# Roots on GpSimd, freely ranked modulations, and a context output that leads the second block

## The chip, the cores and the metric

The kernel runs on one core of one Trainium2 chip. The metric is the device time of one execution in microseconds (us), taken as the median of several runs; lower is better. A core has five instruction streams that run at the same time and meet through semaphores: PE (TensorE, matmuls; its weight loads are shown apart as PEld), DVE (VectorE), ACT (ScalarE), POOL (GpSimd) and SP (SyncE, which here issues the DMAs).

## The reference

All arrays are 32-bit floats; there are 256 tokens of width 1024. The program is two blocks of two layers each, one after the other, cut here to what matters:

```
def first_block(x, mem, ...):                  # DEPTH = 2
    for l in range(2):
        h = rms_norm(x, norm_mix_g[l])         # y * rsqrt(mean(y*y) + 1e-6) * g
        z = h @ w_in[l]                        # three branches: recurrent, mLSTM, memory attention
        ... convolutions, scans, attention ...
        x = x + merged @ w_out[l]
        h2 = rms_norm(x, norm_ffn_g[l])
        x = x + (swiglu(h2, ffn_w1, ffn_w3, ffn_w2) if l == 0 else moe_swiglu(h2, ...))   # 8 experts, 2 per token
    return rms_norm(x, final_norm_g)

def second_block(x, c, ctx, c_ctx, ...):       # DEPTH = 2
    for l in range(2):
        mod_x = split(silu(c) @ ada_w[l] + ada_b[l], 6)       # shift, scale, gate, twice
        mod_c = split(silu(c_ctx) @ ada_w[l] + ada_b[l], 6)
        h_x = rmsnorm(x, g) * (1 + mod_x[1]) + mod_x[0]; h_c likewise from ctx
        o_x, o_c = mixer_ab(h_x, h_c, ...) if l == 0 else mixer_c(h_x, h_c, ...)
        x = x + mod_x[2] * o_x; ... swiglu ...; ctx likewise, for l == 0
    return rmsnorm(x, final_g)
```

In mixer_ab four heads are differential attention (an rms norm over each head's output) and four are neighbourhood attention with a bias table; `o_c = [a_c, b_c] @ w_out_ab` is the context's output, from context tokens alone.

## The kernel before

**Tiling.** Activations lie transposed, features on the 128 partitions, in eight tiles of 256 tokens. Every weight comes from HBM as a block of 1 MB (`load`, L136, issued on SP) into a `raw` buffer; `split` (L144) makes two parts of half a block each, `hi` by a cast on ACT (L149) and `lo = raw - hi` on DVE (L150), and a product is three matmuls (hi by hi, hi by lo, lo by hi; L171 and L175, L190 to L192 where two halves go side by side). There are three `raw` buffers for the whole kernel (`rawps0`) and two more while the experts run (`rawp1`, through `more_raw`), with `self.rawps` the list that `load` goes round.

**Order.** The body is traced in program order, and a scheduler puts each engine's instructions in their final order when the kernel is built: it follows a timeline of its own, and gives an engine that is free the ready instruction of highest rank, where rank is the place in program order. `high_priority(offset=n)` moves the rank of what it encloses forward by n instructions. `issue_after(i)` queues what it encloses, on i's engine, behind i. What is traced inside an `If` stays inside, and what is traced outside can't be mixed into it.

**Roots.** `rsqrt` (L213) computes 1/sqrt(v) for columns of at most [128, 4]: an integer operation for a first guess (L218) and seven more steps on DVE, each waiting for the one before. `spread` (L229) lays a column of 128 values along the free axis of all partitions: a diagonal matrix on DVE (L235), multiplied by ones on PE (L236), one diagonal for each of two groups of 128 tokens. `rms` (L255) and `norm` (L261) use both for every norm; `ctx_tile`, `diff`, `enter` and `leave` use `rsqrt` too.

**Modulations.** `ada_layer` (L1134) makes silu(c) and silu(c_ctx), and `ada(n)` (L1149) takes n of 48 chunks of `ada_w`, transposed: a 512 KB load into one of two `adaw` buffers on SP, and one DVE instruction of 1024 columns for each of c and c_ctx (L1163). The first layer's chunks are traced along the first block's mixers and its feed-forward, the second layer's along the second block's first feed-forward. They stand inside `issue_after(self.last_lo.ins)`, that is, behind the DVE half of the last split traced before them.

**Experts.** `moe` (L1057) runs the eight experts for up to 128 tokens each. Behind them every engine reads the largest count of tokens (L1118) and branches (L1119): if it is over 128, a second body of up to eight more experts follows. With the given inputs it is not, and the body is skipped.

**The second block's first mixer.** `mixer_ab` (L1599) loads the first three quarters of `w_out_ab` (`raw`, FILL = 3), then calls `enter` (L1188), which squares x on ACT (L1197), sums on PE (L1201, 32 small matmuls), takes a root and a spread, and makes the norm `h1`. Three units of the context's output (`ctx_out`, 48 matmuls each, from `o_ctx`, ready since the experts' time) follow, then the heads, woven so that one head's dense products fill the waits of another. `rope` (L1230) ends in one POOL multiply (L1238); `na_bias` (L1441) loads a bias by DMA and, on POOL, multiplies it by 8 (L1455) and adds a mask (L1456).

## Time and profile before

| what | us |
|---|---|
| median of 3 runs (3191.67 to 3192.84) | 3192.14 |
| the profiled execution, its own time | 3190.43 |
| its span, first to last instruction | 3188.6 |
| PE busy in the span | 3094.2 |
| DVE, ACT, POOL busy | 2480.8, 1852.6, 70.1 |
| HBM read | 700.38 MB |

The profile is one execution. A line of the timeline gives the start from the span's beginning, the duration (of several instructions together where xN stands at the end), the engine, the line of the kernel, the operation, out<-in with the program's names, and in brackets the idle time of the engine ahead of it and what ended that. A q behind an engine's name is its instruction queue. The last instruction of the span ends 1.8 us short of the execution's own time.

### The profile page before, as it was taken

To read this page: it belongs to the slowest core of one execution; us is meant where nothing else is said; L and a number is where in the kernel's file an instruction comes from. 1 tells how busy PE (TensorE), PEld (TensorE's weight loads), DVE (VectorE), ACT (ScalarE), POOL (GpSimd) and SP (SyncE) were. 2 spreads that over 40 slices of the span, in tenths; PEclk is the share of its full clock that TensorE was granted. 3 is DMA by queue.
4 is the path that set the end of the run, shared out by engine and by line. 5 is a ranking of instruction groups with operands and counts; after the bars stand their busy time and mean duration, and the time that the engine had idled before them with its cause. 6 is when DMAs were issued, how large, how long until landed. Compare 5 with 4: busy or idle time off the path is not lost. (4 is left out here: it accounts for less than half of the span.)

```text
span 3188.6 us, 53070 instructions
## 1 busy us (share of the span) xinstructions
PE 3094.2 (97%) x21140; PEld 2838.1 (89%) x21140; DVE 2480.8 (78%) x3619; ACT 1852.6 (58%) x2612; POOL 70.1 (2%) x102
## 2 busy tenths in 40 slices
PE   8999999999899999999999999999998999989999
PEld 8899999999899898888888888887988999987999
DVE  7668866678778669999999999997876876676555
ACT  5446644444458457887778878776654222256444
POOL 0000000000000000000000000000320000010000
PEclk9999999999999999999999999999998999999999
DMA  7354656555445559999999999997643444430353
GB/s 273 130 175 159 217 179 219 210 193 213 165 160 180 187 188 345 351 344 348 349 347 335 356 344 341 349 346 241 189 115 128 172 165 166 161 127 31 133 185 119
DMA packets 130873, 712.30 MB, mean 223 GB/s; under 512 B 23352, under 2 KB 35000, under 8 KB 53816
## 3 DMA queue, kind: packets, MB, share of 16 engines
q1 hardware_dynamic: 122552, 701.48, 61.0%
q0 software_dynamic: 8064, 7.34, 1.4%
q8 instruction: 167, 2.74, 0.3%
q14 instruction: 90, 0.74, 0.1%
HBM read 700.38 MB, written 1.05 MB: 220 GB/s over the span
## 5 line engine op out<-in xcount | busy, mean ns | idle before, releaser
L149 ACT CAST hi<-raw 128x1024 fp32r<-128x1024 f32 x1192 | 1233.5, 1051 | 829.7 <-PE ps_a L171 356.6
L150 DVE TENSOR_TENSOR lo<-raw,hi 128x1024 fp32r<-128x1024 f32 x1192 | 1426.5, 1221 | 352.2 <-ACT hi L149 340.0
L171 PE MATMUL ps_a<-hh,hi 128*128 128x256 f32 x2128 | 525.0, 283 | 0.2 <-DVE ks L1261 0.2
L171 PE MATMUL ps_a<-hl,hi 128*128 128x256 f32 x2128 | 524.4, 283 | 0.1
L171 PEld LDWEIGHTS ps_a<-hh,hi 128*128 128x128 f32 x2128 | 401.2, 189 | 4.1 <-issue 2.4
L171 PEld LDWEIGHTS ps_a<-hl,hi 128*128 128x128 f32 x2128 | 401.0, 188 | 3.9 <-issue 3.5
L974 PE MATMUL ps_a<-hi,xsh 128*128 128x512 f32 x896 | 355.0, 396 | 0.0
L975 PE MATMUL ps_a<-hi,xsl 128*128 128x512 f32 x896 | 353.9, 395 | 0.0
L976 PE MATMUL ps_a<-lo,xsh 128*128 128x512 f32 x896 | 351.7, 397 | 0.0
L175 PE MATMUL ps_a<-hh,lo 128*128 128x256 f32 x2128 | 299.3, 282 | 0.0
L175 PEld LDWEIGHTS ps_a<-hh,lo 128*128 128x128 f32 x2128 | 273.8, 188 | 0.5 <-issue 0.4
L825 PE MATMUL ps_b<-gh,lo 128*128 128x256 f32 x752 | 212.3, 283 | 0.0
L824 PE MATMUL ps_b<-gl,hi 128*128 128x256 f32 x752 | 212.1, 283 | 0.0
L823 PE MATMUL ps_b<-gh,hi 128*128 128x256 f32 x752 | 210.5, 283 | 0.0
L975 PEld LDWEIGHTS ps_a<-hi,xsl 128*128 128x128 f32 x896 | 168.3, 188 | 40.0
L976 PEld LDWEIGHTS ps_a<-lo,xsh 128*128 128x128 f32 x896 | 168.3, 188 | 39.5 <-DVE lo L150 0.6
L974 PEld LDWEIGHTS ps_a<-hi,xsh 128*128 128x128 f32 x896 | 168.4, 188 | 37.8 <-issue 0.4
L1006 PE MATMUL ps_b<-hi,mgl 128*128 128x512 f32 x448 | 175.3, 393 | 1.5 <-DVE mgl L992 1.5
L1005 PE MATMUL ps_b<-hi,mgh 128*128 128x512 f32 x448 | 173.8, 391 | 0.0
L825 PEld LDWEIGHTS ps_b<-gh,lo 128*128 128x128 f32 x752 | 144.0, 192 | 0.0
L824 PEld LDWEIGHTS ps_b<-gl,hi 128*128 128x128 f32 x752 | 144.0, 191 | 0.0
L1007 PE MATMUL ps_b<-lo,mgh 128*128 128x512 f32 x448 | 143.8, 396 | 0.0
(564 smaller groups left out, 5675.0 us busy)
## 6 DMA issues: line engine op xcount, KB each, us to landing
raw<-in_moe_w_dram SPq DMA_DIRECT2D x336, 1024.0 KB, 5.9
raw<-in_ffn_w_dram SPq DMA_DIRECT2D x108, 1024.0 KB, 4.8
raw<-in_w_in_dram SPq DMA_DIRECT2D x64, 1024.0 KB, 4.8
adaw<-in_ada_t_dram SPq DMA_DIRECT2D x96, 512.0 KB, 3.8
raw<-in_w_in_ab_dram SPq DMA_DIRECT2D x24, 1024.0 KB, 5.6
raw<-in_w_kv_dram SPq DMA_DIRECT2D x16, 1024.0 KB, 5.0
raw<-in_w_br_xa_dram SPq DMA_DIRECT2D x8, 1024.0 KB, 6.1
raw<-in_w_br_ml_dram SPq DMA_DIRECT2D x8, 1024.0 KB, 4.9
```

Source lines behind the costliest of these rows:

```text
L149: self.last_hi = nc.scalar.copy(hi, view)
L150: self.last_lo = nc.vector.tensor_sub(lo, view, hi.bitcast(F32))
L171: nc.tensor.matmul(out, wh[:, k, :], b[:, k, :], start=start and n == 0, stop=False, skip_group_check=skip)
L175: nc.tensor.matmul(out, wl[:, k, :], xh[:, k, :], start=False, stop=stop and k == nk - 1, skip_group_check=skip)
L823: nc.tensor.matmul(o, wh[:, 0, fs], gh[:, k, :], start=st, stop=False, skip_group_check=True)
L824: nc.tensor.matmul(o, wh[:, 0, fs], gl[:, k, :], start=False, stop=False, skip_group_check=True)
L825: nc.tensor.matmul(o, wl[:, 0, fs], gh[:, k, :], start=False, stop=end, skip_group_check=True)
L974: nc.tensor.matmul(o, xs[0][:, kk, :], wh[:, k, :], start=(kk == 0), stop=False)
L975: nc.tensor.matmul(o, xs[1][:, kk, :], wh[:, k, :], start=False, stop=False)
L976: nc.tensor.matmul(o, xs[0][:, kk, :], wl[:, k, :], start=False, stop=(kk == 7))
L1005: nc.tensor.matmul(o, g[0][:, kk, :], wh[:, 0, ns], start=(c + kk == 0), stop=False)
L1006: nc.tensor.matmul(o, g[1][:, kk, :], wh[:, 0, ns], start=False, stop=False)
```

## The change

It has six parts. (1) `rsqrt` keeps its first step on DVE and does the rest on POOL in ten instructions with immediates only; `spread` makes its diagonals on POOL. (2) The modulations' DVE instructions lose `issue_after` and are ranked 1500 places lower. (3) The `If` behind the experts is told that the path which skips the body is the one to fall through. (4) The loads of the first three quarters of `w_out_ab` move from `mixer_ab` to ahead of that `If`; the body's own loads use the two extra buffers alone. (5) The first unit of the context's output is traced ahead of `enter`. (6) The factor 8 of the bias moves into the table `flip` that the bias is multiplied by on PE, and into the mask; the remaining POOL add is queued behind the last rope multiply.

```diff
@@ -37,6 +37,7 @@
 ADA = 1, 1, 3, 5
+LATER = 1500
 VECS = ["norm_mix_g", "conv_rg_w", "conv_rg_b", "rg_b_a", "rg_b_x", "rg_lambda", "conv_ml_w", "conv_ml_b",
@@ -72,12 +73,12 @@
     ac = (t % 64).astype(np.float32)[:, None] * inv
     ang = np.concatenate([ar, ar, ac, ac], axis=-1).astype(np.float32)
-    parts["flip"] = (p[:, None] // 64 * 64 + 63 - p[:, None] % 64 == p[None, :]).astype(np.float64)
+    parts["flip"] = 8.0 * (p[:, None] // 64 * 64 + 63 - p[:, None] % 64 == p[None, :])
     c = 63 - p % 64
     start = np.clip(c - 8, 0, 48)
     kc = np.arange(64)
     inside = (kc[None, :] >= start[:, None]) & (kc[None, :] < start[:, None] + 16)
-    parts["namask"] = np.where(inside, 0.0, 8 * NEG)
+    parts["namask"] = np.where(inside, 0.0, NEG)
     parts["cos"] = np.tile(np.cos(ang).T, (2, 1))
     parts["sin"] = np.tile(np.sin(ang).T, (2, 1))
     rot = np.zeros((128, 128))
@@ -216,15 +217,20 @@
         nc = self.nc
         t = [self.work.tile([128, 8], F32, name=f"rq{i}", bufs=2)[0:shape[0], 0:shape[1]] for i in range(2)]
         nc.vector.tensor_scalar(t[0].bitcast(I32), v.bitcast(I32), -0.5, float(0x5f3759df), op0=OP.mult, op1=OP.add)
-        nc.vector.tensor_mul(t[1], t[0], t[0])
-        nc.vector.tensor_mul(t[1], t[1], v)
-        nc.vector.scalar_tensor_tensor(t[1], t[1], -10.0 / 3, t[1], op0=OP.add, op1=OP.mult)
-        nc.vector.scalar_tensor_tensor(t[0], t[1], 5.0, t[0], op0=OP.add, op1=OP.mult)
-        nc.vector.tensor_mul(t[1], t[0], t[0])
-        nc.vector.scalar_tensor_tensor(t[1], t[1], -0.5 * 0.375 ** 3, v, op0=OP.mult, op1=OP.mult)
-        nc.vector.scalar_tensor_tensor(t[0], t[1], 1.5 * 0.375, t[0], op0=OP.add, op1=OP.mult)
-        return t[0]
+        pool, (y, w) = nc.gpsimd, t
+        pool.tensor_mul(w, y, y)
+        pool.tensor_mul(w, w, v)
+        u = self.work.tile([128, 8], F32, name="rq2", bufs=2)[0:shape[0], 0:shape[1]]
+        pool.tensor_scalar(u, w, -10.0 / 3, None, op0=OP.add)
+        pool.tensor_mul(u, u, w)
+        pool.tensor_scalar(u, u, 5.0, None, op0=OP.add)
+        pool.tensor_mul(y, y, u)
+        pool.tensor_mul(w, y, y)
+        pool.tensor_mul(w, w, v)
+        pool.tensor_scalar(w, w, -0.5 * 0.375 ** 3, 1.5 * 0.375, op0=OP.mult, op1=OP.add)
+        pool.tensor_mul(y, y, w)
+        return y
     def spread(self, cols):
@@ -232,7 +238,7 @@
         ps = self.bank(self.small)
         for t in range(2):
             dg = self.work.tile([128, 128], F32, name="diag", bufs=2)
-            nc.vector.tensor_scalar(dg, self.ident, cols[:, t:t + 1], None, op0=OP.mult)
+            nc.gpsimd.tensor_scalar(dg, self.ident, cols[:, t:t + 1], None, op0=OP.mult)
             nc.tensor.matmul(ps[:, 0, t * 128:(t + 1) * 128], self.ones[:, :128], dg, start=True, stop=True)
         return ps
@@ -1115,8 +1121,13 @@
         late = []
         self.experts(range(NE), slots.pop, mask, gate, pos, fill=between)
+        self.rawps = self.rawps0
+        self.raw_out = [self.load(self.A["w_out_ab_2"][0], KT, 256, c0=256 * j) for j in range(FILL)]
         most = nc.values_load(count[0:1, NE:NE + 1], min_val=0, max_val=S)
-        with tc.If(most > 128):
+        with tc.If(most > 128, preferred_fallthrough_block=False):
+            self.rawps = self.rawps1
             for e in range(NE):
                 n = nc.values_load(count[0:1, e:e + 1], min_val=0, max_val=S)
                 with tc.If(n > 128):
@@ -1124,6 +1135,7 @@
                     for fn in steps:
                         fn()
                     self.experts([e], lambda e: xs[e % 2], mask, gate, pos, 128)
+        self.rawps = self.rawps0
     def ada_setup(self):
@@ -1155,7 +1167,8 @@
             l, c = self.ada_left.pop(0)
             raw = self.adap.tile([128, D], F32, name="adaw", bufs=2)
             nc.sync.dma_start(raw, self.A["ada_t"][l, 128 * c:128 * c + 128])
-            with self.tc.issue_after(self.last_lo.ins):
+            with self.tc.high_priority(offset=-LATER):
                 for name, s in self.silu.items():
                     if name == "c_ctx_2" and l == 1 and c >= 16:
                         continue
@@ -1235,7 +1248,7 @@
         pr = bank[:, 1, :]
         nc.tensor.matmul(pr, self.late["rot"], t, start=True, stop=True)
         nc.vector.tensor_mul(m, pr, self.late["sin"])
-        nc.gpsimd.tensor_mul(t, t, self.late["cos"])
+        self.last_rope = nc.gpsimd.tensor_mul(t, t, self.late["cos"])
         nc.vector.tensor_add(t, t, m)
         return t
@@ -1452,8 +1465,8 @@
                                       bass.AP(tensor=rpb.tensor, offset=off + h * 465, ap=[[1, 64], [31, 4], [1, 64]]))
         m = self.late["namask"][:, None, :].to_broadcast([128, 16, 64])
         v = b.rearrange("p t h i c -> p (t h i) c")
-        nc.gpsimd.tensor_scalar(v, v, 8.0, None, op0=OP.mult)
-        nc.gpsimd.tensor_add(v, v, m)
+        with self.tc.issue_after(self.last_rope.ins):
+            nc.gpsimd.tensor_add(v, v, m)
         return b
     def tables_of(self, first, last):
@@ -1600,7 +1613,12 @@
         nc, A = self.nc, self.A
         w, wo = A["w_in_ab_2"][0], A["w_out_ab_2"][0]
         self.tg = TG
-        raw = [self.load(wo, KT, 256, c0=256 * j) for j in range(FILL)]
+        def out(s, j, o, raw=None):
+            self.add_mod(s, 0, 0, j, self.proj2(wo, 256 * j, o, raw=raw))
+        ctx_out = [lambda j=j: out(0, j, self.o_ctx, self.raw_out[j] if j < FILL else None) for j in range(4)]
+        ctx_out[0]()
         h = self.enter()
         late = self.late = self.tables_of("flip", "rot")
         oT = self.act_pair("o")
@@ -1654,12 +1672,7 @@
             return [self.attend(Q[g], b, ks, vs, 2 * f + b, put, more(b)) for b in range(2)]
-        def out(s, j, o, raw=None):
-            self.add_mod(s, 0, 0, j, self.proj2(wo, 256 * j, o, raw=raw))
-        ctx_out = [lambda j=j: out(0, j, self.o_ctx, raw[j] if j < FILL else None) for j in range(4)]
-        for fn in ctx_out[:FILL]:
+        for fn in ctx_out[1:FILL]:
             fn()
         groups = [(dense(0), lambda: jobs(0))]
         for g in range(1, 8):
@@ -1833,7 +1846,8 @@
     def more_raw(self, ctx, name, n):
-        self.rawps = self.rawps0 * RAW + [ctx.enter_context(self.tc.tile_pool(name=name, bufs=n))] * n
+        self.rawps1 = [ctx.enter_context(self.tc.tile_pool(name=name, bufs=n))] * n
+        self.rawps = self.rawps0 * RAW + self.rawps1
     def first(self):
         tc, A = self.tc, self.A
```

## Rows read from the trace of the kernel before

**Rows 1.** The page: busy time of each engine

```profile
PE 3094.2 (97%) x21140; PEld 2838.1 (89%) x21140; DVE 2480.8 (78%) x3619; ACT 1852.6 (58%) x2612; POOL 70.1 (2%) x102
```

**Rows 2.** Stages: busy us of each engine (instructions), clock, DMA share, GB/s

```profile
50.00:100.00 50.00, 50.00 (x396) 49.07 (x395) 32.58 (x44) 23.47 (x37) 0.00 (x0) 1.00 0.56 206
2205.00:2222.00 17.00, 10.99 (x53) 10.71 (x52) 5.96 (x15) 9.21 (x18) 1.16 (x2) 0.60 0.68 228
2500.00:2550.00 50.00, 50.00 (x421) 50.00 (x421) 43.98 (x72) 11.76 (x14) 0.00 (x0) 1.00 0.51 174
```

**Rows 3.** Timeline of PE, 2205 to 2248: start, us, operation, [idle before <-releaser]

```profile
2205.18 0.28 PE L1023 MATMUL ps_b<-sct,yl 128*128 128x256 f32 x1
2210.49 6.98 PE L1201 MATMUL ps_b<-squared,sq 128*128 128x2 f32 x32 [5.03 <-ACT sq L1197]
...
2240.02 0.28 PE L171 MATMUL ps_a<-h1h,hi 128*128 128x256 f32 x1
...
2247.20 0.38 PE L429 MATMUL ps_a<-hi,h1h 128*128 128x256 f32 x1 [1.35 <-ACT hi L149]
```

**Rows 4.** The If's line L1119: its branches and waits, by engine's queue: ns min/median/max

```profile
L1119 DVEq EVENT_SEMAPHORE  x2: 21/21/21, 2209.4 to 2209.5; - x2
...
L1119 PEldq COMPARE_BRANCH  x1: 3882/3882/3882, 2205.3 to 2205.3; - x1
L1119 DVEq COMPARE_BRANCH  x1: 72/72/72, 2206.5 to 2206.5; - x1
```

**Rows 5.** Timeline of ACT: the context output's first weights

```profile
2217.36 1.99 ACT L149 CAST hi<-raw 128x1024 fp32r<-128x1024 f32 x2 [1.76 <-DMA raw<-in_w_out_ab_dram]
```

**Rows 6.** Timeline of PE: sixteen one-column sums late in the kernel

```profile
3178.78 1.95 PE L251 MATMUL ps_b<-consts,sq 128*128 128x1 f32 x16 [1.57 <-DVE sq L247]
```

**Rows 7.** Timeline of DVE in the second mixer, 806 to 818

```profile
806.39 1.21 DVE L1163 SCALAR_TENSOR_TENSOR prod<-adaw,silu_c 128x1024 f32<-128x1024 f32 x1
...
812.21 0.73 DVE L344 TENSOR_SCALAR cv<-pad,vecs 128x256 f32<-128x256 f32 x2
...
817.33 1.22 DVE L1163 SCALAR_TENSOR_TENSOR prod<-adaw,silu_c_ctx 128x1024 f32<-128x1024 f32 x1
```

**Rows 8.** Timeline of PE: the wait that this stretch ends in, in both mixers

```profile
150.79 0.58 PE L171 MATMUL ps_b<-hi,half 128*128 128x256 f32 x1 [5.40 <-ACT half L368]
...
822.36 0.58 PE L171 MATMUL ps_b<-hi,half 128*128 128x256 f32 x1 [8.74 <-ACT half L368]
```

**Rows 9.** Timeline of DVE: a root with nothing beside it, 2978 to 2980

```profile
2978.66 0.16 DVE L219 TENSOR_TENSOR rq<-rq 128x2 f32<-128x2 f32 x1
...
2980.03 0.48 DVE L235 TENSOR_SCALAR diag<-consts,rq 128x128 f32<-128x128 f32 x2
```

**Rows 10.** Timeline of PE: waits for the spread of such roots

```profile
1100.64 1.22 PE L236 MATMUL ps_b<-diag,consts 128*128 128x128 f32 x4 [3.79 <-DVE diag L235]
...
2980.37 1.22 PE L236 MATMUL ps_b<-diag,consts 128*128 128x128 f32 x4 [2.14 <-DVE diag L235]
```

**Rows 11.** POOL's own durations: the rope multiply, the memset, the two bias operations

```profile
L1238 POOL TENSOR_TENSOR rt<-rt,late x18: 722/740/1453, 2250.7 to 2916.2; 128x256 f32<-128x256 f32 x18
...
L352 POOL MEMSET pad<- x16: 103/104/108, 0.7 to 953.2; 128x6 f32 x16
...
2229.86 2.85 POOL L1455 TENSOR_SCALAR bias<-bias 128x1024 f32<-128x1024 f32 x1 [12.93 <-DMA bias<-in_na_rpb_dram]
2232.79 2.39 POOL L1456 TENSOR_TENSOR bias<-bias,late 128x1024 f32<-128x1024 f32 x1
```

**Rows 12.** Timeline of DVE and PE: the root and its spread after the first attention

```profile
2404.64 0.16 DVE L218 TENSOR_SCALAR rq<-ms 128x2 int32<-128x2 int32 x1
...
2420.22 0.77 PE L236 MATMUL ps_b<-diag,consts 128*128 128x128 f32 x2 [5.83 <-DVE diag L235]
```

**Rows 13.** Timeline of POOL and DVE: where the two meet, 2233 to 2252

```profile
2250.67 1.45 POOL L1238 TENSOR_TENSOR rt<-rt,late 128x256 f32<-128x256 f32 x1 [2.49 <-PE ps_a L1236]
...
2233.36 1.90 DVE L235 TENSOR_SCALAR diag<-consts,rq 128x128 f32<-128x128 f32 x1
```

## The prediction, made before the result was known

> **What bounds the kernel now.** I read the page first: PE is busy 3094.2 of 3188.6 us, 97% [rows 1], so only what PE waits for, and what its clock loses, is to be had. The windows by stage say where. In the experts and the feed-forward blocks PE is busy in the whole window, with 421 matmuls of 128x256 in 50 us, 0.119 us each [rows 2]; there DVE work costs nothing as long as the weight splits keep ahead. PE stands still only where one stage hands over to the next, so I went through PE's timeline there, then looked at DVE's and POOL's at the same moments. The reader is to see four places: the handover from the experts to the second block [rows 3], a wait of 5.40 us in the first mixer and of 8.74 us in the second one at the same line [rows 8], and the waits for L236, the spread of a root over partitions [rows 10, 12].
>
> **Part 1: handover from the experts (branch, early weights, first unit leads).** PE ends the experts at 2205.18 + 0.28 = 2205.46 and starts the first matmul of h1 at 2240.02 [rows 3]: 34.6 us. Its own work in between, at the full clock: three context-output units of 48 matmuls, 144 x 0.119 = 17.1 us [rows 2]; 32 sums, which late in the kernel took 1.95 us for sixteen [rows 6], so 3.9 us against the 6.98 us here [rows 3]; two spreads of 1.22 us [rows 10], 2.4 us. That is 23.4 us, and 11.2 us are lost. They are lost to three things. The skip over the experts' second body is a taken branch: PE's own COMPARE_BRANCH lasts 3.88 us, and DVE, whose branch stands at 2206.5, is back at 2209.4 [rows 4]. Then PE has nothing to do, because the context output's weights are issued behind the If and ACT gets the first of them at 2217.36 [rows 5]. Third, the mean granted clock from 2205 to 2222 is 0.60 [rows 2], close to the lower of its two levels (1.2 and 2.4 GHz), after this idle stretch. With the loads ahead of the If, ACT can cast the first weights while DVE still adds to x, and PE's first unit, 5.7 us, covers squares, sums and root. I leave 2 us for the root's chain, so this gives back 9 us, and the wait of 1.35 us for a weight at 2247.20 [rows 3] goes too, since raw buffers come free earlier: -10 us. Bounds: -4 (only the branch) and -13 (all of it). SP has to issue three 1 MB loads ahead of its branch and ahead of the late table and the bias DMAs; they wait for raw buffers of the last expert, and nothing that PE needs is behind them. If they landed late, the first cast would wait as it does now [rows 5].
>
> The Trainium skill, page "Runtime: NRT & Kernel Launch", section "Instruction fetch mechanics", says that a taken branch to a target outside the prefetched pages stalls on a fetch; the 3.88 us row agrees in kind, and by that rule the fall-through would drop the whole stall.
>
> **Part 2: modulations without issue_after, ranked low.** There are 160 such instructions, each 1.2 us on DVE. Today they are held behind the last split of their unit, and let go in a burst. In the second mixer six of them start between 806.39 and 817.33, three after the first convolution step at 812.21 and one just ahead of it [rows 7]; the half that PE waits 8.74 us for [rows 8] hangs on those steps. Three are 3.7 us, with a part of the fourth 4.5 us. Free to run, they fill DVE's idle time from the start: from 50 to 100 us DVE is busy 32.58 of 50 us [rows 2], so all 96 of the first layer (117 us) fit ahead of the second mixer: -4.5 us. Their 512 KB loads move forward with them on SP's queue; the DMA share there is 0.56 [rows 2]. But a low rank doesn't hold a ready instruction back when DVE has nothing else, so the same steps of the first mixer, 5.40 us of wait today [rows 8], will now be filled: three gaps between dependent steps of at most 1.2 us, 3.7 us at worst, zero or a small gain at best (one group stands there already). I take +1. Sum: -3.5 us, bounds -7 and +4.
>
> **Part 3: roots and diagonals on POOL.** Eight DVE operations become one on DVE and ten on POOL; two diagonals per spread move too. No row shows so small an operation on POOL. From below the nearest is the memset of six columns, 0.104 us; from above the multiply of 256 columns, 0.722 us at its fastest [rows 11]. With the 1024-column one at 2.39 us the line through both meets zero columns near 0.17 us; two dependent POOL operations start 0.08 us after one another's end (2229.86 + 2.85 against 2232.79) [rows 11]. I take 0.26 us for each step, near the line's foot because two columns are next to none: 2.6 us for ten, against 2980.03 - 2978.66 = 1.37 us on DVE [rows 9], so +1.3 us. A diagonal of 128 columns is then about 0.5 us against half of 0.48 us [rows 9], +0.6 us for a pair. Where DVE has nothing else and PE waits, this is all on the path: at 1100.64 and 2980.37 [rows 10], 1.9 us each, and at the last root, +1.3 us, of which some hides under the last transposes. Part 3a: +5 us; bounds 0 (steps like the memset) and +12 (steps of 0.5 us). The other roots lie beside PE's work; that is their cover, and the queue of POOL behind a root (rope multiplies, key copies, bias adds) has room: POOL is busy 70.1 us in all [rows 1].
>
> After the first attention DVE is crowded: the root begins at 2404.64, its steps take turns with splits, and PE waits 5.83 us for the spread until 2420.22 [rows 12]. On POOL the steps no longer queue behind DVE's, but they meet them at the memory: the rope multiply took 1.45 us instead of 0.74 where DVE ran a two-operand split beside it, and a diagonal on DVE took 1.90 us beside POOL's bias add [rows 13]. So a step costs 0.26 to about 1.3 us there, ten steps 2.6 to 13 us; at about 9 us the spread comes some 5 us earlier. Part 3b: -4 us, bounds -9 and +2.
>
> The Trainium skill, page "SBUF — State Buffer", section "SBUF: two separate sides", says the pair of ports that DVE shares with GpSimd is an exclusive lock for a whole instruction; that speaks against putting roots there, and the 1.45 us row agrees. By it alone every step would wait for a split, and part 3b would be zero.
>
> **Smaller edits.** The bias loses one POOL operation of 2.8 us four times [rows 11], off PE's path; its add now stands behind the last rope multiply and is wanted only by the later heads' scores. What waits behind it on POOL are key copies, as now. The factor 8 goes into two tables at no cost.
>
> **The sum.** -10 - 3.5 + 5 - 4 = -12.5 us on the profiled run's own 3190.43 us, 3177.9 us. The median of the runs is 1.7 us above that run: about 3180 us.
>
> **Rivals.**
> Roots cost more than they save: slower. If POOL's dependent steps take 0.8 us (as if two columns cost what 256 do), each idle root is 8 - 1.37 + 0.6 = 7.2 us longer; three make +21 us, part 3b gives 0 and part 1 only -7 us: -7 - 3.5 + 21 = +10.5, 3203 us. It cancels the gains from about 0.55 us a step. For it: the meetings of [rows 13] and the 0.722 us minimum; against: the memset and the line's foot. Chance 0.17.
> The modulations come back elsewhere: with nothing to hold them they fill the first mixer's chain (+3.7), the first feed-forward's norm (+2), and, for the second layer, the norm after the attention, so that part 3b gives 1: -10 + 5.7 - 4.5 + 5 - 1 = about -5, 3187 us. For it: a ready instruction is taken when DVE is free [rows 7]; against: DVE's idle share early on. Chance 0.20.
> The handover doesn't move: the loads land late or the order puts x's squares behind the casts so that the root ends where it ends today. Part 1 then gives -3: 3187 us. Chance 0.13.
> The forecast itself: 0.50, with 3171 to 3186 as its own range.
>
> **How the numbers follow.** A measurement of this kernel tells about 0.2%, 6.4 us, from no change: faster is below 3185.8, slower above 3198.5. Faster holds nearly all of the forecast (0.46) and parts of the second and third rival (0.12): 0.58. Slower is most of the first (0.14) and the far ends of the others (0.03): 0.17. The rest, 0.25, is the same. The range runs from part 1 and 3b at their better bounds, 3166, to the unfavourable middle of the first rival, 3199.
>
> **What would show it.** Right: PE's branch row short; the first o_ctx matmul within 3 us of the experts' end, first h1 matmul near 2230; no modulation near the second mixer's convolutions and that wait at 4 us or so; POOL's root steps 0.2 to 0.35 us where DVE is idle; PE's wait at L236 about 2 us longer there and shorter after the attention. Wrong: root steps above 0.5 us, or the first mixer's wait grown as much as the second's shrank.

## The result and the profile after

The changed kernel takes 3228.17 us (median of 4 runs, 3223.31 to 3232.47), the kernel before 3191.90 in the same comparison: a ratio of 1.0114, interval 1.0094 to 1.0134. It is 36 us slower. The forecast was 3180 us with a range up to 3199: the sign was wrong and the time lies outside the range. The profiled execution took 3232.47 us. The page after, busy time of each engine [rows 1]:

```profile
PE 3095.0 (96%) x21140; PEld 2834.6 (88%) x21140; DVE 2457.4 (76%) x3448; ACT 1849.2 (57%) x2612; POOL 159.8 (5%) x332
```

PE's busy time is that of before (3094.2), while the span grew from 3188.6 to 3230.7: what was added, in sum, is time in which PE stands still. Both kernels issue 21140 matmuls, so I took the start of PE's n-th matmul in one trace less that of the n-th in the other, all along. The fourth column anticipates the experiments: e5 is the kernel before, with every tile where the changed kernel has it and nothing else changed.

| matmul | at, in before, us | after less before | after less e5 | what lies in the stretch that ends here |
|---|---|---|---|---|
| 800 | 114 | +4.8 | +5.6 | first norms |
| 1600 | 226 | +31.7 | +33.9 | the first mixer's chains |
| 6800 | 893 | +16.5 | +26.1 | first feed-forward, second mixer's convolutions |
| 13600 | 2153 | +18.4 | +32.2 | spread at 1112 us, experts |
| 14400 | 2291 | +28.3 | +40.2 | handover to the second block |
| 15600 | 2469 | +34.2 | +45.9 | norms behind the first attention |
| 19200 | 2930 | +40.6 | +52.1 | start of the last mixer |
| 20800 | 3140 | +40.0 | +53.8 | last feed-forward |

The largest step is in the first mixer. Busy time by stage there (PE, PEld, DVE, ACT and POOL with their instructions, PE's clock, DMA share, GB/s), first of the kernel before, then of the changed one:

```profile
140.00:160.00 20.00, 14.60 (x81) 13.36 (x81) 12.09 (x22) 9.37 (x15) 0.10 (x1) 0.83 0.25 80
160.00:180.00 20.00, 20.00 (x154) 18.36 (x153) 12.54 (x20) 8.38 (x13) 0.00 (x0) 1.00 0.50 174
```

```profile
140.00:160.00 20.00, 8.57 (x41) 6.71 (x39) 19.75 (x39) 1.47 (x2) 0.00 (x0) 0.68 0.49 170
160.00:180.00 20.00, 7.17 (x22) 5.39 (x23) 18.98 (x39) 6.87 (x16) 0.00 (x0) 0.67 0.41 142
```

PE falls from 34.60 to 15.74 us of 40 while DVE rises from 24.63 to 38.73. What DVE does, and what PE waits for (timelines of the changed kernel, DVE from 144 us, then PE), with the count of the modulations from 140 to 180 us ahead of them (ns min/median/max):

```profile
L1176 DVE SCALAR_TENSOR_TENSOR prod<-adaw,silu_c x12: 1148/1222/1229, 141.0 to 179.8; 128x1024 f32<-128x1024 f32 x12
...
L1176 DVE SCALAR_TENSOR_TENSOR prod<-adaw,silu_c_ctx x11: 1187/1206/1226, 142.5 to 178.1; 128x1024 f32<-128x1024 f32 x11
```

```profile
144.74 0.40 DVE L301 SCALAR_TENSOR_TENSOR r<-r,r 4x256 f32<-4x256 f32 x1
145.07 1.20 DVE L1176 SCALAR_TENSOR_TENSOR prod<-adaw,silu_c 128x1024 f32<-128x1024 f32 x1
...
146.21 0.41 DVE L301 SCALAR_TENSOR_TENSOR r<-r,r 4x256 f32<-4x256 f32 x1
146.55 1.21 DVE L1176 SCALAR_TENSOR_TENSOR prod<-adaw,silu_c_ctx 128x1024 f32<-128x1024 f32 x1
...
147.69 0.41 DVE L301 SCALAR_TENSOR_TENSOR r<-r,r 4x256 f32<-4x256 f32 x1
...
154.62 0.37 PE L419 MATMUL ps_b<-consts,r 4*128 4x4 f32 x2 [9.37 <-DVE r L411]
...
162.66 3.78 PE L496 MATMUL ps_b<-xpt,xv 128*128 128x256 f32 x8 [3.11 <-ACT xpt L492]
...
179.46 0.58 PE L172 MATMUL ps_b<-hi,half 128*128 128x256 f32 x1 [9.49 <-ACT half L374]
```

Twenty-three modulations run here, where the kernel before has two (at 139.7 and 140.9 us); one of 1.2 us has slipped in between every two steps of a dependent chain of 0.4 us steps (here the series for the mLSTM's gates). The wait of [rows 8] in this mixer went from 5.40 to 9.49 us, and two more, 9.37 and 3.11 us, were not there before.

Where the forecast looked, the rows read as follows. The wait of the second mixer [rows 8] fell from 8.74 to 4.96 us, as said. The two spreads of idle roots [rows 10], and POOL's steps at the first of them:

```profile
1114.39 0.19 POOL L221 TENSOR_TENSOR rq<-rq 128x2 f32<-128x2 f32 x1 [145.15 <-DVE rq L219]
1114.66 0.20 POOL L222 TENSOR_TENSOR rq<-rq,ms 128x2 f32<-128x2 f32 x1
...
1117.25 1.19 POOL L241 TENSOR_SCALAR diag<-consts,rq 128x128 f32<-128x128 f32 x2
...
1117.91 1.38 PE L242 MATMUL ps_b<-diag,consts 128*128 128x128 f32 x4 [5.66 <-POOL diag L241]
...
3022.93 1.38 PE L242 MATMUL ps_b<-diag,consts 128*128 128x128 f32 x4 [3.99 <-POOL diag L241]
```

A step comes every 0.28 us (ten in 2.86), and the waits are 1.87 and 1.85 us longer than 3.79 and 2.14. At the handover, the branches of the If (line 1128 now; ns min/median/max) and PE after them:

```profile
L1128 PEldq COMPARE_BRANCH  x2: 95/1719/3343, 2223.5 to 2224.1; - x2
```

```profile
2227.54 0.58 PE L172 MATMUL ps_a<-o_ctxh,hi 128*128 128x256 f32 x1 [3.74 <-ACT hi L150]
...
2260.32 0.80 PE L172 MATMUL ps_a<-h1h,hi 128*128 128x256 f32 x2 [7.11 <-ACT h1h L286]
...
2261.92 0.58 PE L172 MATMUL ps_a<-h1l,hi 128*128 128x256 f32 x1 [0.59 <-DVE h1l L287]
...
2267.76 0.58 PE L172 MATMUL ps_a<-h1l,hi 128*128 128x256 f32 x1 [2.49 <-DVE h1l L287]
```

PE now has two branches: the conditional one lasts 95 ns, and right behind it a second one, the jump over the body, lasts 3343 ns, where the one of before lasted 3882 [rows 4]. The stall has moved, it has not gone. h1 starts 2260.32 - 2223.80 = 36.5 us behind the experts' last matmul; before it was 34.6.

### The profile page after: what moved, and what is told of

Same layout as the page of the kernel before. It is cut to its first block, busy times and chain, and to the rows that moved or that the text cites. A ratio compares the mean times of both kernels' runs of the same rounds, so it can differ in the third digit from the quotient of the medians.

```text
span 3230.7 us, 53169 instructions
## 1 busy us (share of the span) xinstructions
PE 3095.0 (96%) x21140; PEld 2834.6 (88%) x21140; DVE 2457.4 (76%) x3448; ACT 1849.2 (57%) x2612; POOL 159.8 (5%) x332
## 5 line engine op out<-in xcount | busy, mean ns | idle before, releaser
L829 PEld LDWEIGHTS ps_b<-gh,hi 128*128 128x128 f32 x752 | 143.1, 191 | 1.7 <-DVE ctx L1236 1.7
```

The source lines that it names most:

```text
L829: nc.tensor.matmul(o, wh[:, 0, fs], gh[:, k, :], start=st, stop=False, skip_group_check=True)
```

## The experiments

Parts are numbered as in the prediction: part 1 is the handover (early loads, fall-through, first unit ahead), part 2 the freed modulations, part 3 the roots and diagonals on POOL. The table has medians, beside the kernel before on the same chip (3191.0 to 3191.9 us in every comparison).

| run | what it is | us | ratio to before, interval |
|---|---|---|---|
| e1 | before + part 2 (modulations free) | 3236.21 | 1.0135, 1.0119 to 1.0150 |
| e2 | before + part 3 (roots on POOL) | 3180.11 | 0.9964, 0.9951 to 0.9978 |
| e3 | before + part 1 (handover) | 3195.87 | 1.0012, 1.0003 to 1.0021 |
| e4 | after, part 2 undone | 3192.24 | 1.0001, 0.9992 to 1.0010 |
| e5 | before, tiles 64 bytes higher | 3174.60 | 0.9942, 0.9928 to 0.9955 |
| e6 | before, tiles 32 bytes higher | 3169.65 | 0.9928, 0.9914 to 0.9941 |
| e7 | e3 + bias DMAs behind weights | 3191.71 | 1.0002, 0.9993 to 1.0011 |
| e8 | before, modulations moved by count | 3186.69 | 0.9986, 0.9977 to 0.9995 |
| e9 | e2 + bias edit | 3183.52 | 0.9971, 0.9959 to 0.9984 |
| e10 | e6 + e8 | 3162.56 | 0.9909, 0.9894 to 0.9924 |
| e11 | e10 + two roots on POOL | 3162.73 | 0.9905, 0.9890 to 0.9921 |
| e12 | e10 + bias DMAs behind weights | 3161.35 | 0.9904, 0.9889 to 0.9920 |
| e13 | e1, modulations on a quarter | 3202.86 | 1.0041, 1.0026 to 1.0057 |
| e14 | e1, held in the first mixer | 3222.53 | 1.0099, 1.0084 to 1.0115 |
| e15 | before, tiles 96 bytes higher | 3126.62 | 0.9793, 0.9779 to 0.9806 |
| e16 | weights 64 and h 96 bytes higher | 3168.41 | 0.9936, 0.9922 to 0.9949 |
| e17 | pair tiles 64, h 96 higher, e8 | 3129.16 | 0.9805, 0.9792 to 0.9819 |
| e18 | e17 + bias DMAs behind weights | 3129.55 | 0.9810, 0.9796 to 0.9823 |

### Which part costs: e1 to e4

e1, part 2 alone:

```diff
-            with self.tc.issue_after(self.last_lo.ins):
+            with self.tc.high_priority(offset=-LATER):
```

> The kernel before with part 2 alone (the modulations lose issue_after and get the low rank). Theory: in the trace of the changed kernel one modulation of 1.2 us stands between nearly every two dependent DVE steps of the first mixer from 140 to 180 us, and PE is busy 15.7 us of these 40 instead of 34.6; later, where the modulations are then missing, some 11 us come back. Alone it should cost 10 to 16 us: 3202 to 3208 us, with PE's two waits of over 9 us before 180 us there again. Rival (the roots on POOL make the first mixer late, and the modulations only fill what is idle anyway): within 4 us of the kernel before, and no wait over 6 us in the first mixer.

It cost 44.5 us, some three times as much, and the rival fell: with the roots on DVE the same chains are broken up. The first wait of over 9 us is there again; the second came to 6.69 us only. PE's rows:

```profile
159.98 0.37 PE L414 MATMUL ps_b<-consts,r 4*128 4x4 f32 x2 [9.68 <-DVE r L406]
...
183.82 0.58 PE L172 MATMUL ps_b<-hi,half 128*128 128x256 f32 x1 [6.69 <-ACT half L369]
...
2453.21 0.77 PE L237 MATMUL ps_b<-diag,consts 128*128 128x128 f32 x2 [8.29 <-DVE diag L236]
...
2462.45 0.80 PE L191 MATMUL ps_a<-h_ctxh,hi 128*128 128x256 f32 x2 [4.64 <-ACT h_ctxh L281]
```

Counted by matmuls it stands +35.5 us behind the kernel before at 226 us, +26.9 at 893 us, and then loses 16 us more at the norms behind the first attention, where the second layer's modulations are free too; my expectation had left these out, and had taken the give-back from the changed kernel, where half of it was something else (e5).

e2, part 3 alone (`rsqrt` and `spread` as in the change):

> The kernel before with part 3 alone (roots and diagonals on POOL). Theory: an idle root with its spread takes 4.05 us on POOL against 2.05 us on DVE, and a crowded step 1.0 to 1.3 us, so the first norm loses some 5 us, the two idle spreads 2 us each and the norms of the last mixer some 5: 10 to 15 us slower, 3202 to 3207 us. Rival (as forecast, the roots cost 5 us and give back 4 after the attention): 3191 to 3195 us.

It was 11.6 us faster, outside both. The matmuls of the feed-forward came faster, without any wait in either kernel; e5 takes this apart.

e3, part 1 alone:

> The kernel before with part 1 alone (fall-through, early loads, first unit ahead). Theory: the late resource of this handover is the first w_in_ab block, which lands 31 us behind the experts' end in both traces because its issue on SP stands behind the bias DMAs; so the context units are moved forward and PE then waits for h1's weights: between 6 us faster and 6 us slower, 3186 to 3198 us, with a wait of 4 to 8 us ahead of h1. Rival (h1 is late in the changed kernel because the root takes 8.7 us on POOL): the root is back on DVE here, so 6 to 10 us faster, 3182 to 3186 us, and h1 starts within 28 us of the experts' end.

4.2 us slower (interval 1 to 7), within the theory's range, with a wait of 8.70 us ahead of h1, a little over the 4 to 8 expected, and h1 40 us behind the experts' end, though the root is on DVE; the rival fell. The rows that decide, of SP, ACT and DVE:

```profile
2214.28 11.78 SPq L1456 DMA_DIRECT2D bias<-in_na_rpb_dram  x10
2226.17 1.01 SPq L141 DMA_DIRECT2D raw<-in_w_in_ab_dram  x2
...
2234.69 1.04 ACT L149 CAST hi<-raw 128x1024 fp32r<-128x1024 f32 x1 [9.42 <-DMA raw<-in_w_in_ab_dram]
...
2235.77 2.92 DVE L150 TENSOR_TENSOR lo<-raw,hi 128x1024 fp32r<-128x1024 f32 x1 [6.51 <-ACT hi L149]
2238.60 2.36 DVE L235 TENSOR_SCALAR diag<-consts,rq 128x128 f32<-128x128 f32 x1
2240.88 2.47 DVE L272 TENSOR_TENSOR xg<-xg,ps_b 128x512 f32<-128x512 f32 x4
```

The weights of h1 are issued behind ten bias DMAs, land at 2234.69, and DVE, whose order has their split ahead of the norm's multiplies, stands idle for 6.51 us with the root long done.

e4, the changed kernel with part 2 undone:

> The changed kernel with part 2 undone (the modulations are held behind the last split again). Theory: takes back what e1 costs, 10 to 18 us: 3210 to 3218 us, still slower than the kernel before through roots and handover. Rival (the modulations cost only because of POOL's roots, or the roots because of them): 3195 us or less.

3192.24 us: all 36 us come back. The number is the rival's, its reason is not: in e1 the modulations cost as much with the roots on DVE. What my expectation had wrong is how much of the loss this part carries, since the roots and the handover stand on a better placing here (e5) than in the kernel before; with it they come out level with that.

### The placing: e5, e6, e15, e16, e17

The changed `rsqrt` has a third temporary, `rq2`, two buffers of 32 bytes in a partition, and with it the tiles allocated behind it on that side of SBUF lie 64 bytes higher: in the built programs the activations h begin at byte 107168 of a partition instead of 107104, while the weight halves, the raw blocks and the pair tiles (`pair` pool: among others the feed-forward's gated product) stay where they are. e5 does only that (the order of the instructions is unchanged):

```diff
+        self.work.tile([128, 8], F32, name="rq2", bufs=2)
```

> The kernel before with nothing but an unused tile of two times 32 bytes in the work pool, where the changed rsqrt has its third temporary: every later tile lies 64 bytes higher, as in the changed kernel, and the order of the instructions on each engine is that of the kernel before. Theory: in e2 PE's matmuls of 128x256 in the first feed-forward come every 118.3 ns and in the kernel before every 119.9 ns, without any wait in either, and the placing of the operands in SBUF is what differs: this kernel shows 118.3 ns too and is 8 to 12 us faster, 3180 to 3184 us. Rival (the steadier rate comes from DVE doing less, the roots being on POOL): 119.9 ns and no change, 3190 to 3193 us.

> The kernel before with an unused tile of 32 bytes, so that every later tile lies 32 bytes higher (the activations h start at a multiple of 128 bytes instead of 96 bytes past one; with 64 bytes they start 32 past one). Theory of the placing: the spacing of the 128x256 matmuls in the first feed-forward changes again, to anything from 116 to 120 ns, 3172 to 3192 us. Rival (placing is of no matter): 119.9 ns, 3190 to 3193 us.

> A third placing: an unused tile of 96 bytes in the work pool, so that the activations h start 64 bytes past a multiple of 128 (96 in the kernel before, 32 in e5, 0 in e6). The order of the instructions is that of the kernel before. Theory: the distance of h from a multiple of 128 bytes is what counts and the kernel before has the worst of the four: 3168 to 3185 us with matmuls every 117 to 119 ns in the first feed-forward. Rival (only e5's and e6's placings are good, by something else that moved): 3186 to 3195 us.

e6 has `bufs=1`, e15 a tile of 96 bytes. All three are faster, by 16.8, 21.8 and 64.8 us, so the placing counts. The rival fell each time, and each time the gain was beyond my range, e15's far beyond. In the first feed-forward, where PE waits for nothing, the stages read (kernel before, e5, e6, e15):

```profile
500.00:670.00 170.00, 170.00 (x1419) 170.00 (x1418) 112.40 (x130) 72.76 (x78) 0.00 (x0) 1.00 0.60 212
```

```profile
500.00:670.00 170.00, 170.00 (x1441) 170.00 (x1440) 113.30 (x131) 74.16 (x80) 0.00 (x0) 1.00 0.61 217
```

```profile
500.00:670.00 170.00, 170.00 (x1431) 170.00 (x1430) 112.47 (x130) 73.15 (x79) 0.00 (x0) 1.00 0.61 215
```

```profile
500.00:670.00 170.00, 170.00 (x1473) 170.00 (x1471) 117.61 (x137) 77.90 (x89) 0.00 (x0) 1.00 0.60 217
```

PE is busy throughout at a clock of 1.00 and gets through 1419, 1441, 1431 or 1473 matmuls. A matmul here streams 256 columns of activations past weights that were loaded before: hh and hl are the two parts of h, gh and gl those of the gated product, which lie in pair tiles. By the operand that they stream (mean from one start to the next, 500 to 670 us; addresses in bytes past a multiple of 128):

| kernel | h at | weight halves at | pair tiles at | ns, matmuls with hh, hl | ns, with gh, gl |
|---|---|---|---|---|---|
| before | 96 | 0 | 0 | 117.0, 120.2 and 122.8 | 119.8 |
| e5 (and the changed kernel's placing) | 32 | 0 | 0 | 117.4 | 119.8 |
| e6 | 0 | 0 | 0 | 118.7 | 119.6 |
| e15 | 64 | 0 | 0 | 113.5 | 119.6 |
| e16 | 64 | 64 | 64 | 118.7 | 119.6 |
| e17 | 64 | 0 | 64 | 117.7 | 117.9 |

In the experts the matmuls of 512 columns with xsh and xsl, the two parts of the chosen tokens, go from 233.3 ns in the kernel before to 227.7 in e15 (1400 to 1800 us, steps over 260 ns left out as waits). Is it where h lies by itself, or where it lies against other tiles? e16 has e6's tile and moves the weights too:

```diff
+            self.padp = pool("padp", 1)
+            self.padp.tile([128, 16], F32, name="padp")
             self.hip = pool("hip", 4)
```

> The order of the kernel before, the activations h at the same addresses as in e15 (64 bytes past a multiple of 128), but the weight halves hi and lo, the raw blocks and the pair tiles (gh, gl) are 64 bytes higher as well: an unused tile of 64 bytes ahead of them and one of 32 in the work pool. Theory A (what counts is where h lies by itself): the matmuls with h stay at 113.5 ns, about 3127 us, or less if gh and gl, now 64 bytes past a multiple of 128 too, gain as well. Theory B (what counts is h against the weights that are loaded beside it): both lie at the same distance again as in e6, so about 118.6 ns and 3165 to 3175 us.

```profile
500.00:670.00 170.00, 170.00 (x1431) 170.00 (x1430) 112.16 (x130) 73.82 (x80) 0.00 (x0) 1.00 0.61 215
```

Theory B: h is at the address of e15, the weights have moved under it, and the rate is e6's to the tenth of a nanosecond, 3168.41 us. So it is not where h lies by itself that counts, but where it lies against something else. That this is the weights is not shown: in e16 the raw blocks and the pair tiles moved together with the weight halves. The Trainium skill, page "TensorE: Matmul & The Clock Gate", section "Step-by-step: what each phase is for", says that loading the next tile's weights takes no SBUF read bandwidth from the running matmul. The runs show a spacing that changes by some 5% with the placing (120.0 ns on the mean before, 113.5 in e15), but not that it is the loading of weights that the stream meets, so they don't settle this.

e17 puts the pair tiles 64 bytes off too (the same pool ahead of `pair`) and adds e8's ADA.

> h at 64 bytes past a multiple of 128 as in e15, the weight halves at a multiple of 128 as in the kernel before, the pair tiles (gh and gl in the feed-forward, mgh and mgl in the experts) moved to 64 bytes past one by an unused tile of 64 bytes ahead of them, and the modulations of e8. Theory: the 2256 matmuls with gh or gl go from 119.8 to some 113.5 ns as those with h did, 14 us, and e8's 5 us come on top of e15: 3104 to 3114 us. Rival (the pair tiles' rate hangs on something else than the address): 3119 to 3125 us.

This missed: 3129.16 us, no better than e15. gh and gl gained only 2 ns; hh and hl lost 4 in the first feed-forward, not in the last (113.4 there), though h and the weight halves lie where e15 has them; and the experts' matmuls with mgh and mgl, the gated product there, went from 227.2 to 233.4 ns. The modulations that e17 brings into the first feed-forward are hardly the reason: with the same ones the spacing with hh and hl is 120.0 ns in e8 as in the kernel before, and 118.7 in e10 as in e6. What is left is the pair tiles' place, for matmuls that don't read them. And no distance is good everywhere: in the experts the chosen tokens lie 32, 64 and 0 bytes past the weights' place modulo 128 in the kernel before, e6 and e15, at 233.3, 229.8 and 227.7 ns, so that 0 is the best there and nearly the worst in the feed-forward. The distance modulo 128 is not the rule, and what is stays open.

### How the modulations cost: e13, e14, e8, e10

e13 keeps the loads and shortens the instruction:

```diff
-                    nc.vector.scalar_tensor_tensor(pr, raw, 1.0, s, ...
+                    nc.vector.scalar_tensor_tensor(pr[:, :256], raw[:, :256], 1.0, s[:, :256], ...
```

> e1 with each modulation on 256 of its 1024 columns (the sums are left incomplete; the loads stay at 512 KB and come as early as in e1). Theory: e1 loses its time because DVE gives 1.2 us to a modulation between every two short dependent steps; at some 0.4 us each two thirds of the loss goes: 3200 to 3212 us, and PE's waits before 180 us fall to about a third. Rival (the modulations' loads, which now run together with the weights', are what is late): within 6 us of e1, 3230 to 3242 us.

3202.86 us: 33 of e1's 44.5 us go, for two thirds of the DVE time, and PE's two waits of 9.68 and 6.69 us become 2.34 and 6.00 (the second was 5.40 in the kernel before). It is the time on DVE that costs; the loads are the smaller part, if any.

e14 holds them in the first mixer alone:

> e1, but in the first block's first mixer the modulations are held behind the last split as before; from the first feed-forward on they are free and ranked low. Theory: the 31 to 35 us that e1 loses up to 226 us are this stage's, the 16 us around the norms behind the second block's first attention and the few in its feed-forward stay: 3202 to 3212 us. Rival (the free modulations find the next chain of dependent steps in the first feed-forward's norm or the second mixer instead): 3215 us or more.

Here the rival was right: 3222.53 us. The first mixer loses nothing (-0.4 us at 226 us), and the next chains of dependent steps, from 405 to 462 us, lose 19: PE waits 4.17, 8.66, 4.10 and 2.04 us there, where the kernel before has 1.89 and 2.32. The second of these is for the root of the first feed-forward's norm, on DVE:

```profile
446.69 0.15 DVE L222 SCALAR_TENSOR_TENSOR rq<-rq 128x2 f32<-128x2 f32 x1
446.76 1.22 DVE L151 TENSOR_TENSOR lo<-raw,hi 128x1024 fp32r<-128x1024 f32 x1
447.90 0.15 DVE L224 SCALAR_TENSOR_TENSOR rq<-rq,rq 128x2 f32<-128x2 f32 x1
448.05 1.22 DVE L1166 SCALAR_TENSOR_TENSOR prod<-adaw,silu_c 128x1024 f32<-128x1024 f32 x1
...
449.20 0.15 DVE L225 TENSOR_TENSOR rq<-rq 128x2 f32<-128x2 f32 x1
449.32 1.22 DVE L1166 SCALAR_TENSOR_TENSOR prod<-adaw,silu_c_ctx 128x1024 f32<-128x1024 f32 x1
```

In e1 that stage lost nothing: the first layer's modulations were used up by 267 us. The cost goes to whichever chain is running while any are left.

e8 gets the one gain that was sought, by count: `ADA = 1, 3, 0, 5`, with issue_after kept.

> The kernel before with issue_after as it was and ADA = 1, 3, 0, 5: the 24 chunks of modulations that stood in the second mixer are taken in the first feed-forward instead, each still behind a split. Theory: the second mixer's wait of 8.74 us falls to about 5 and nothing is late in the first feed-forward, where DVE has idle time: 3 to 6 us faster, 3186 to 3189 us. Rival (three chunks, 7.2 us of DVE in a burst, make the splits of the feed-forward late): 3192 to 3200 us.

> e6 and e8 together: every later tile 32 bytes higher and the modulations of the second mixer moved to the first feed-forward, still behind splits. Theory: the two don't touch each other, 21.8 + 4.7 us under the kernel before: 3163 to 3167 us. Rival (the gain of one of them hangs on the planner's order or on a wait that the other removes): 3168 us or more.

e8 gave 4.7 us (the second mixer's wait is 4.96 us), and with e6's placing the two add up to within 3 us: 3162.56.

### The queue ahead of h1: e7, e12, e18

```diff
+                with self.tc.issue_after(self.last_load.ins):
                     for h in range(2):
                         nc.sync.dma_start(b[par * 64:(par + 1) * 64, t, h],
```

`last_load` is the last weight DMA traced before.

> e3 (part 1 alone) with one edit more: the bias DMAs are queued on SP behind the last weight load traced before them, so that the w_in_ab loads no longer stand behind sixteen bias issues. Theory: h1's wait of 8.7 us in e3 is for these weights and for the DVE splits that are ordered ahead of the norm's multiplies; with the loads issued as soon as a buffer is free they land by 25 us behind the experts' end, PE's wait falls under 3 us and the kernel is 8 to 13 us faster than e3: 3183 to 3188 us. Rival (the norm's chain on DVE or POOL's bias work is what is late, or the later heads now wait for the bias): within 4 us of e3, 3192 to 3199 us.

> e10 with the bias DMAs queued behind the weight loads on SP, without part 1. Theory: h1's first cast waits 3.5 us for its weights in the kernel before as well, and this wait goes; what e7 lost again with the later heads may come too: 0 to 5 us faster than e10. Rival (the later heads' bias, now late, costs more than h1's wait): 1 to 6 us slower than e10.

> e17 with the bias DMAs queued on SP behind the weight loads (as e12 beside e10). Theory: 0 to 5 us faster than e17. Rival (the later heads wait for the bias as long as h1 did for its weights): within 1 us of e17 or slower.

In e7 no wait over 0.4 us is left between 2207.53 and 2270 us, so what was late is shown. But of the 11 us that it was ahead of e3 at matmul 14400, 5 were lost again 400 matmuls on, among the later heads: 3191.71 us, 4 us better than e3, between the two ranges, and level with the kernel before. e12 and e18 can't be told from e10 and e17.

### Roots: e9, e11

> The kernel before with roots and diagonals on POOL and the bias edit (its add queued behind the last rope multiply), but neither part 1 nor part 2; between e2 (3180.1 us, roots alone) and e4 (3192.2 us, the same and part 1 too). Theory: the 12 us between these two are part 1's, whose wait for h1 and the stretch of low clock behind it are in e4's trace and not in e2's; so this kernel stays with e2: 3177 to 3184 us. Rival (the bias add queued behind a rope multiply holds up POOL's roots and key copies in the second block): 3188 to 3193 us.

3183.52 us: within the theory's range, so the bias edit (3.4 us with intervals that overlap) can't be told from nothing, and the larger part of the 12 us between e2 and e4 is part 1's.

e11 has roots on POOL only for the two norms behind the first attention, `onpool` being set around them:

```diff
+        if self.onpool:
+            pool, (y, w) = nc.gpsimd, t
...
-            nc.vector.tensor_scalar(dg, self.ident, ...
+            (nc.gpsimd if self.onpool else nc.vector).tensor_scalar(dg, self.ident, ...
```

> e10 with roots and diagonals on POOL for two norms alone, those behind the second block's first attention, where DVE is crowded; the temporary that this needs is the 32 bytes of e6. Theory: in e2 against e5, which have the same placing, this stretch is 4.3 us shorter and the rest 3 to 5 us longer, so this kernel is 3 to 5 us faster than e10: 3158 to 3163 us, with PE's wait at the first of these spreads under 2 us. Rival (the gain there came from other DVE work being in another place): within 1.5 us of e10.

PE's wait there, in e10 and in e11:

```profile
2396.90 0.76 PE L237 MATMUL ps_b<-diag,consts 128*128 128x128 f32 x2 [6.00 <-DVE diag L236]
```

```profile
2390.49 0.49 PE L253 MATMUL ps_b<-diag,consts 128*128 128x128 f32 x2 [2.73 <-POOL diag L252]
```

The wait fell as in e2, though not under the 2 us expected; the gain didn't come, as the rival's range has it: 3162.73 us. By matmuls e11 gains 3.7 us at these norms and loses 4.8 again at the start of the last mixer, which both kernels compute alike. The stage there, e10 and then e11:

```profile
2760.00:2860.00 100.00, 90.29 (x678) 85.06 (x677) 74.24 (x161) 57.68 (x125) 10.39 (x15) 0.93 0.32 106
```

```profile
2760.00:2860.00 100.00, 89.62 (x641) 84.67 (x641) 71.57 (x155) 55.47 (x118) 11.41 (x15) 0.90 0.31 106
```

PE is busy about as long, at a mean granted clock of 0.93 and 0.90, which over 100 us would be 3 of the 4.8 us, an estimate. That this is how the gain went I take from these rows alone; no run here sets the clock by itself.

## Why the prediction was wrong, step by step

On one placing, that of the changed kernel, the medians can be taken apart: e5 3174.6, with the roots 3180.1 (e2), with the bias edit 3183.5 (e9), with the handover 3192.2 (e4), with the free modulations 3228.2. So the parts cost +5.5, +3.4, +8.7 and +36.0 us, 53.6 in all, and 16.8 of this were hidden by the placing, which the change brought without meaning to. Single runs of each of these kernels spread over 5 to 9 us, and the same differences between the profiled executions are +1.4, +5.3, +4.0 and +45.5: the last is clear of the noise, the size of the others is not.

**Part 2, forecast -3.5, bounds -7 and +4; +36.0 alone in this company, +44.5 by itself.** This is the step that decided. "Three gaps between dependent steps of at most 1.2 us" was counted on the one chain that ended in the wait of [rows 8]. The stage holds several chains one behind the other, the gates' series above all, which PE's work covered before and which therefore ended no wait. The 23 modulations between 140 and 180 us are 23 x 1.2 = 27.6 us. The idle time that I had pointed to, 32.58 busy of 50 us in [rows 2], was free: in the changed kernel it took nineteen modulations instead of six, and PE lost nothing there:

```profile
50.00:100.00 50.00, 50.00 (x402) 49.25 (x401) 45.99 (x68) 22.81 (x34) 0.00 (x0) 1.00 0.72 245
```

But by 140 us only 38 of the 96 had run. "All 96 fit ahead of the second mixer" came true (the last starts at 275 us) and was the wrong test, since the first mixer's chains lie on the way. Between the steps of a chain the idle time belongs to the chain: a queue in order hands it to the next ready instruction at the price of its whole length. The second mixer's gain was right (-3.8 against -4.5). The second layer's modulations, on the norms behind the attention, I named in the second rival, and priced that rival at a fifth of what it was.

**Part 1, forecast -10; +8.7, and +4.2 alone.** Two steps failed. The fall-through was to make the branch short: it did, and the jump behind it took over the stall, 3343 of 3882 ns. The Trainium skill's rule that I cited (page "Runtime: NRT & Kernel Launch", section "Instruction fetch mechanics") would hold for the jump as well, and the 3343 ns agree in kind, though no run here shows the fetch; I had applied it to one branch of two. And "a stall goes": I didn't ask what was late next. In the kernel before, too, ACT waits for the w_in_ab weights, 31 us behind the experts' end:

```profile
2236.87 1.05 ACT L149 CAST hi<-raw 128x1024 fp32r<-128x1024 f32 x1 [3.49 <-DMA raw<-in_w_in_ab_dram]
```

That row was there to be read. I had written that nothing that PE needs stands behind the early loads on SP; the w_in_ab loads need the same three buffers, and stand behind sixteen bias DMAs. The early loads did their part, ACT casts at 2225.49, 1.7 us behind the experts, against 12 [rows 5]; this only moved the idle time behind the three units, in one piece, with the clock at 0.53 from 2256 to 2274 us.

**Part 3a, forecast +5, and 3b, -4; together +5.5 for +1.** The sizes were right: 0.28 us a step for 0.26, 1.87 and 1.85 us at the two idle spreads for 1.9, and behind the attention the wait fell from 5.62 (e5) to 2.89 us (e2), some 4 us by matmuls. Of ten crowded steps there six took 1.0 to 1.3 us, as bounded from [rows 13], and each of the six ends with the two-operand instruction that DVE runs beside it. The first of them (POOL, then DVE, in the changed kernel):

```profile
2435.38 1.10 POOL L221 TENSOR_TENSOR rq<-rq 128x2 f32<-128x2 f32 x1 [30.90 <-DVE rq L219]
...
2435.21 1.22 DVE L151 TENSOR_TENSOR lo<-raw,hi 128x1024 fp32r<-128x1024 f32 x1
```

By the Trainium skill's rule of the lock (page "SBUF — State Buffer", section "SBUF: two separate sides") POOL waits for such an instruction to end, and these rows agree.

What failed is "the other roots lie beside PE's work": the one ahead of the last mixer does not, and PE's first waits there rose from 1.82 and 1.47 us to these:

```profile
2849.72 0.39 PE L191 MATMUL ps_a<-h_ctxh,hi 128*128 128x256 f32 x1 [4.32 <-ACT h_ctxh L286]
...
2853.75 0.58 PE L192 MATMUL ps_a<-h_ctxl,hi 128*128 128x256 f32 x1 [3.53 <-DVE h_ctxl L287]
```

Some 3 us that e2 loses to e5 along the experts I can't place.

**What no step counted: -16.8.** A temporary of 64 bytes. The price of a matmul, 0.119 us from [rows 2], was taken as given, and it is the largest term of the whole kernel. That this gain fell into the change, and brought its time nearer to the range, was luck.

**Rivals and signs.** Of the rivals the first (a root's step dearer than 0.55 us) fell, the third (the handover doesn't move) came nearest for part 1, and the second named the mechanism that decided. Of the signs, the first o_ctx matmul came 3.74 us behind the experts, for 3, and h1 36.5 us behind them, for 25. The sign for "wrong", the first mixer's wait grown as much as the second's shrank, came: +4.09 against -3.78 us. One sum in the prediction doesn't come out: part 1 and 3b at their better bounds give -20.5 us and 3172 us, not 3166; nothing hung on it.

## What to carry to other kernels

Idle time of an in-order engine may lie between the steps of a dependent chain, and then it isn't free; before filling it, count the steps of every chain in that stage, covered ones too, since each can pay the filler's whole length, and place fillers by count where no chain runs (e8) rather than by a low rank. When a stall is removed, follow the next operand back to the queue that issues it. And when an experiment adds or drops a tile, run the same addresses without the edit first: here the addresses were worth more than the edit, and an unused tile of 96 bytes, 64.8 us (2%), is the best kernel found.

## What the hardware showed that I had not expected

- The spacing of matmuls in an unbroken stream depends on where the tiles lie in SBUF against one another: for 128x256 in the first feed-forward, 113.5 ns with h 64 bytes past the weights modulo 128 (e15), 117.4 at 32 (e5), 118.7 at 0 (e6, and e16 with both moved), and 117.0 to 122.8 at 96 (before). No rule is shown: the pair tiles' place changes 113.5 to 117.7 (e17), and the experts have another best distance (227.7 ns at 0).
- A conditional branch made to fall through leaves a jump, and the jump stalled PE for 3.34 us (3.80 in e3), where the branch of before took 3.88.
- Small operations on POOL are cheap: 0.19 us for two columns, 0.28 us from start to start in a chain, and 1.0 to 1.3 us when DVE runs a two-operand instruction such as a split beside them.
